# Output projection by Strassen's scheme, token-major, with its sum transposed and x added by VectorE; all 22 inner blocks of down in the scheme

## The chip, the cores and the metric

One core of one Trainium2 chip. Five engines matter: TensorE (PE; PEld is its weight load), VectorE (DVE), ScalarE (ACT), GpSimd (POOL) and SyncE (SP), whose queue issues most DMAs. The metric is device microseconds of one launch.

## What is computed

One decoder layer for 512 tokens, model width 1024, FFN width 2816. The reference, cut to what matters here (the head splits and the two attentions are left out):

```python
h = rms_norm(x, g_mix[layer])
proj = h @ w_in[layer]
...
g = jax.nn.sigmoid(gates + b_gate[layer]).reshape(b, s, N_BRANCHES, D_MODEL)
merged = g[:, :, 0] * (ya @ w_branch_a[layer]) + g[:, :, 1] * (yb @ w_branch_b[layer])
x = x + merged @ w_out[layer]
h = rms_norm(x, g_ffn[layer])
u = causal_depthwise_conv(h @ w_up[layer], conv_w[layer], conv_b[layer])
u_gate, u_val = jnp.split(u, 2, axis=-1)
x = x + (jax.nn.silu(u_gate) * u_val) @ w_down[layer]
return rms_norm(x, g_final)
```

## The kernel before

Every large product is made of three fp32r matmuls, hi by hi, hi by lo, lo by hi (`mm3`, L71 to L74). Weights come as tiles of 128 x 1024 fp32 (`raw`, five buffers, on SP's queue); ScalarE copies the high half (`whi`), VectorE subtracts the low half (`wlo`): `wload` L55 to L69, `split_w` L602 to L609, `split_out` (L262, L263) for activations.

Stages: input projection, the two attentions, then per output block of 128 features the gate projections (16 blocks, held back as fillers for TensorE, L452) and the two gated products `ab` (`mm<-ya`, `mm<-yb`, L496 to L504). Their sum is split into `m`.

**Output projection** (L512 to L527): feature-major, for each of 8 output blocks 8 inner blocks x 3 matmuls of 512 columns into one PSUM bank. VectorE adds the bank to x (`x1T`, L516); ScalarE and VectorE make the halves of `h2` (L517, L518); ScalarE stores x1 to DRAM (L520) and squares it (L522), VectorE adds the squares up (L526). Behind the first up block eight passes against a vector of ones sum the squares over the features (L117).

**Up** (L532 to L590): 44 blocks of 24 matmuls, two to each of the 22 inner blocks (FT). Per block: VectorE's product with the norm's factor (`u`, L559), ScalarE's first tap (L561), VectorE's two other taps (L562, L564). Of a pair of inner blocks (j) the first 9 (NP) go to `tm` and `xb`, four sums and a split into `xa`, the left operands of a Strassen scheme (L576 to L582); the last four inner blocks (18 to 21) go to `gT` unchanged (L569).

**Down**, token-major, eight PSUM banks of 128 tokens x 512 features (c11 to c22, each two blocks of 128 tokens). First pass, per j of 9: two weight loads, two subtractions (L620, L621), a copy (L622), two splits, and the four products c22, c21, c11, c12 of 6 matmuls each. Then the sums u2, u3 (L650 to L661). Second pass, per j: a subtraction (L642), a weight split, the splits of `xs` and `w4` (L263), prepared two steps ahead, and three products of 6. At j = 6 the residual x1, read back from DRAM feature-major (`x1R`), is added by 32 transposes on TensorE (L684). Then 96 plain matmuls for `gT`, 128 tokens after 128 tokens, each half followed by its ending: Square with row sum (L699), product with the gain (L701), square root (L704), reciprocal and corrections, scaling (L712, L714), store (L715).

TensorE's order is that of the code (`manual_schedule`); a scheduler orders the instructions of the other engines. A buffer's next writer waits for its last reader.

Of the kernel before, what the change touches and what calls it, by code (L numbers as in the profile page):

```python
# [10 lines left out]
F32 = mybir.dt.float32  # L11
# [16 lines left out]
NP = 9  # L28
# [3 lines left out]
          + [("out", i) for i in range(KT)] + [("up", i, b) for i in range(FT) for b in range(2)]  # L32
# [6 lines left out]
def trunk_layer(ctx: ExitStack, tc: tile.TileContext, xT: bass.AP, w: bass.AP, vec: bass.AP,  # L39
# [46 lines left out]
    warmb = consts.tile([128, 448], BF, name="warmb")  # L86
    nc.vector.memset(warmb, 0.0)
# [55 lines left out]
    xp = pool(st1, "xp", 6)  # L143
    p1 = pool(st1, "p1", 1, PSUM)
# [471 lines left out]
    for j in range(NP):  # L616
# [9 lines left out]
        if j == NP - 1:  # L626
            steps = steps[2:] + steps[1::-1]
# [155 lines left out]
```

## Time and profile before

| | |
|---|---|
| median of 3 runs | 731.37 us (731.29 to 731.92) |
| the profiled execution | 731.76 us, span 730.0 us |
| granted TensorE clock, mean | 0.997 |
| PE / PEld / DVE / ACT / POOL busy | 722.6 / 601.0 / 511.1 / 326.7 / 22.9 us |
| chain that ended last | PE 99% |
| DMA | 80.95 MB, mean 111 GB/s |

Busy time is read as a share of the span; the chain of waits is followed back from the last instruction, at each step to what released it. A matmul of 512 columns lasts 0.39 us in the trace and overlaps the next; what counts is the distance between starts. Durations below are of the profiled execution.

### The profile page before, as it was taken

What the parts mean: (1) busy time and instruction counts of PE and PEld (TensorE: products, weight loads), DVE (VectorE), ACT (ScalarE), POOL (GpSimd) and SP (SyncE); (2) the same over time, 40 slices, a digit from 0 to 9 for tenths busy, and PEclk for the clock granted to TensorE, in tenths of its full rate; (3) what the DMA queues carried; (4) which work ended last, traced back from release to release, by engine and by line L of the source; (5) the groups of instructions that cost most, each with busy time, mean ns of one, the idle gap of its engine ahead of it and who ended that gap; (6) DMA issues with size and microseconds to landing.
All of it is one profiled execution on the core that took longest, in us unless ns stands there. A gap on an engine that the chain in (4) does not pass through costs nothing.

```text
span 730.0 us, 9687 instructions
## 1 busy us (share of the span) xinstructions
PE 722.6 (99%) x3836; PEld 601.0 (82%) x3836; DVE 511.1 (70%) x724; ACT 326.7 (45%) x468; POOL 22.9 (3%) x40
## 2 busy tenths in 40 slices
PE   9999999999999999999999999999999999999996
PEld 6887889889888888888888888888888888888885
DVE  7778866693963644446548788877778888889913
ACT  6335544563663323224335444434444445466623
POOL 0000000320410000000000000000000000000000
PEclk9999999999999999999999999999999999999998
DMA  8422111021225232233432232232232223568303
GB/s 310 186 87 87 58 59 59 30 88 58 85 91 173 89 113 87 92 110 125 147 132 87 86 115 88 87 116 87 91 112 87 95 79 115 193 216 294 105 1 115
DMA packets 25389, 80.95 MB, mean 111 GB/s; under 512 B 2816, under 2 KB 3456, under 8 KB 25344
## 3 DMA queue, kind: packets, MB, share of 16 engines
q1 hardware_dynamic: 23472, 77.06, 31.3%
q10 hardware_dynamic: 1872, 3.28, 1.2%
q8 instruction: 30, 0.49, 0.3%
q14 instruction: 15, 0.12, 0.0%
HBM read 76.13 MB, written 4.19 MB: 110 GB/s over the span
## 4 chain that ended last, share of the span: by engine, by line
PE 99%; DVE 0%; issue 0%; ACT 0%; DVEq 0%; ACTq 0%
PE mm L72 24%; PE mm L74 23%; PE mm L73 23%; PE c L72 5%; PE c L74 5%; PE c L73 5%; PE q L187 3%; PE tp L428 2%; PE tp L406 2%; PE sc L329 1%; PE sc L339 1%; PE mm L149 0%; PE v L74 0%; PE v L72 0%; PE v L73 0%; PE c L684 0%
## 5 line engine op out<-in xcount | busy, mean ns | idle before, releaser
L67 ACT ACTIVATE whi<-raw 128x1024 fp32r<-128x1024 f32 (+2 forms) x106 | 106.9, 1012 | 212.3 <-PE mm L73 130.9
L72 PE MATMUL mm<-h,whi 128*128 128x512 f32 x352 | 137.1, 390 | 0.0
L74 PE MATMUL mm<-h,wlo 128*128 128x512 f32 x352 | 137.0, 389 | 0.0
L73 PE MATMUL mm<-h,whi 128*128 128x512 f32 x352 | 136.9, 389 | 0.0
L68 DVE TENSOR_TENSOR wlo<-raw,whi 128x1024 fp32r<-128x1024 f32 (+2 forms) x106 | 122.8, 1163 | 15.8 <-ACT whi L67 15.5
L72 PE MATMUL mm<-xg,whi 128*128 128x512 f32 x224 | 90.0, 402 | 0.0
L74 PE MATMUL mm<-xg,wlo 128*128 128x512 f32 x224 | 87.5, 390 | 0.0
L73 PE MATMUL mm<-xg,whi 128*128 128x512 f32 x224 | 87.3, 390 | 0.0
L73 PEld LDWEIGHTS mm<-h,whi 128*128 128x128 f32 x352 | 66.1, 188 | 13.8
L74 PEld LDWEIGHTS mm<-h,wlo 128*128 128x128 f32 x352 | 66.1, 188 | 13.7
L72 PEld LDWEIGHTS mm<-h,whi 128*128 128x128 f32 x352 | 66.1, 188 | 13.6
L559 DVE TENSOR_TENSOR u<-mm,rb 128x512 f32<-128x512 f32 x44 | 30.3, 691 | 30.5 <-PE mm L74 30.4
L72 PEld LDWEIGHTS mm<-xg,whi 128*128 128x128 f32 x224 | 42.1, 188 | 10.2 <-issue 1.8
L74 PEld LDWEIGHTS mm<-xg,wlo 128*128 128x128 f32 x224 | 42.0, 188 | 9.1
L73 PEld LDWEIGHTS mm<-xg,whi 128*128 128x128 f32 x224 | 42.2, 188 | 7.8
L607 ACT ACTIVATE whi<-raw 128x1024 fp32r<-128x1024 f32 x31 | 31.9, 1050 | 23.5 <-DVE raw L620 14.3
L608 DVE TENSOR_TENSOR wlo<-raw,whi 128x1024 fp32r<-128x1024 f32 x31 | 37.3, 1220 | 3.6 <-ACT whi L607 3.6
L561 ACT ACTIVATE t<-u,vecs 128x512 f32<-128x512 f32 x44 | 35.2, 803 | 2.0 <-DVE u L559 2.0
L452 DVE TENSOR_TENSOR g<-mm,rb 128x512 f32<-128x512 f32 x16 | 11.0, 688 | 34.4 <-PE mm L74 34.4
L564 DVE SCALAR_TENSOR_TENSOR t<-u,vecs,t 128x510 f32<-128x510 f32 x44 | 32.9, 749 | 1.3
L562 DVE SCALAR_TENSOR_TENSOR t<-u,vecs,t 128x511 f32<-128x511 f32 x44 | 32.8, 747 | 1.4 <-ACT t L561 1.3
L567 ACT ACTIVATE t<-t 128x512 f32<-128x512 f32 x22 | 13.8, 628 | 35.5 <-DVE t L564 35.5
(202 smaller groups left out, 1271.9 us busy)
## 6 DMA issues: line engine op xcount, KB each, us to landing
raw<-w SPq DMA_DIRECT2D x127, 512.0 KB, 3.3
xk<-xT SPq DMA_DIRECT2D x8, 256.5 KB, 5.3
x1T<-xT SPq DMA_DIRECT2D x8, 256.0 KB, 5.0
x1D<-x1T ACTq DMA_DIRECT2D x8, 256.0 KB, 2.0
x1R<-x1D SPq DMA_DIRECT2D x4, 512.0 KB, 7.5
raw<-w SPq DMA_DIRECT2D x6, 256.0 KB, 5.5
out<-on ACTq DMA_DIRECT2D x4, 256.0 KB, 2.5
out<-on SPq DMA_DIRECT2D x4, 256.0 KB, 2.7
```

Of the source, the lines that this page charges most:

```text
L67: nc.scalar.activation(hi[:, sl], raw[:, sl], AF.Copy)
L68: nc.vector.tensor_sub(lo[:, sl], raw[:, sl], hi[:, sl].bitcast(F32))
L72: nc.tensor.matmul(ps, a[0], b[0], start=start, stop=False, **kw)
L73: nc.tensor.matmul(ps, a[0], b[1], start=False, stop=False, **kw)
L74: nc.tensor.matmul(ps, a[1], b[0], start=False, stop=stop, **kw)
L187: nc.tensor.matmul(qk0[c], w0[i][:, (k % 2) * 512 + c * 128:(k % 2) * 512 + (c + 1) * 128], xg[k][:, j], start=(k == 0 and n == 0), stop=( ...
L559: nc.vector.tensor_mul(u, ps, rb2)
L561: nc.scalar.activation(t, u, AF.Identity, bias=cb[:, c:c + 1], scale=cw[:, 2, c:c + 1])
L562: nc.vector.scalar_tensor_tensor(t[:, 1:], u[:, :S - 1], cw[:, 1, c:c + 1], t[:, 1:], op0=OP.mult, op1=OP.add)
L564: nc.vector.scalar_tensor_tensor(t[:, 2:], u[:, :S - 2], cw[:, 0, c:c + 1], t[:, 2:], op0=OP.mult, op1=OP.add)
L607: nc.scalar.activation(hi, raw, AF.Copy)
L608: nc.vector.tensor_sub(lo, raw, hi.bitcast(F32))
```

## The change

The output projection takes the scheme that down has, in pairs of inner blocks (HP = 4): `a_side` makes `oa` and `ob` from the gated sums, `first_pass` and `sums` are shared with down, the second pass is written out, c12's products last. The result is token-major in eight banks (`po`). x comes in token-major (a new input) and VectorE adds it (`x1_add`); `x1_turn` transposes 256 tokens x 512 features back (8 transposes a time) and ScalarE and VectorE make `h2` from PSUM. The squares are summed by ScalarE token by token (`x1_sq`). x1 is stored by SP's queue. In down all 11 pairs are in the scheme, `gT` and the plain matmuls are gone, VectorE adds the residual (`residual`), and the last three steps (NL) of the second pass are held: c21's 18 matmuls, the endings of tokens 256 to 511, then the four other banks, 9 matmuls each, with their endings. `u` has one buffer instead of two, small constants move to other pools, and `spare` takes the place of the pool `ptr2`, with no tile taken from it.

```diff
-NP = 9
+NP = FT // 2
+NL = 3
...
+    warmb = xp.tile([128, 448], BF, name="warmb", bufs=1)
+    nc.vector.memset(warmb, 0.0)
...
-    ptr = pool(psB, "ptr2", 2, PSUM)
+    spare = pool(psB, "spare", 2, PSUM)
     pmm = pool(psB, "pmm2", 6, PSUM)
...
+    def a_side(odd, put, tm, xa, xb):
+        if not odd:
+            put(tm[:, 0::4])
+            return
+        put(xb[:, 0::2])
+        nc.vector.tensor_add(tm[:, 1], tm[:, 4], xb[:, 2])
+        nc.vector.tensor_sub(tm[:, 3], tm[:, 0], tm[:, 4])
+        nc.vector.tensor_sub(tm[:, 2], tm[:, 1], tm[:, 0])
+        nc.vector.tensor_sub(xb[:, 1], xb[:, 0], tm[:, 2])
+        split_out(xa.rearrange("p a b c -> p a (b c)"), tm[:, :4].rearrange("p b c -> p (b c)"))
...
-        nc.vector.tensor_add(g[0], g[0], g[1])
-        split_out(mhl[i], g[0])
+        if i % 2 == 0:
+            tm = mtp.tile([128, 5, 256], F32, name="tm")
+        g0, g1 = (u.rearrange("p (t c) -> p t c", t=2) for u in g)
+        a_side(i % 2, lambda dst: nc.vector.tensor_add(dst, g0, g1), tm, oxa[i // 2], oxb[i // 2])
...
-    for i in range(KT):
-        wo = wload(("out", i))
-        ps = pmm.tile([128, S], F32, name="mm")
-        for k in range(KT):
-            mm3(ps, blk(wo, k), (mhl[k][:, 0], mhl[k][:, 1]), k == 0, k == KT - 1)
-        nc.vector.tensor_add(x1T[i], x1T[i], ps)
-        nc.scalar.activation(h2[i][:, 0], x1T[i], AF.Copy, scale=gffn[:, i:i + 1])
...
+    for t in range(QT):
+        nc.sync.dma_start(x1[:, t], x[t * 128:(t + 1) * 128])
...
+    for j in range(HP):
+        first_pass(oq, j, HP, oxa[j], (("ox", j), ("out", 2 * j)), t2[j], slots[j], True)
...
+    second = [oprep(j, (wsp, osp, osp)[j]) for j in range(3)]
+    w4s = [oprep4(j) for j in range(2)]
+    last, lact = sums(oq, ocb)
...
+    def x1_add(t, h):
+        sl = slice(h * 512, (h + 1) * 512)
+        ins = nc.vector.tensor_add(x1[:, t, sl], x1[:, t, sl], oq[f"c{t // 2 + 1}{h + 1}"][t % 2])
+        nc.sync.dma_start(x1D[t][:, sl], x1[:, t, sl])
+        return ins
+
+    def x1_turn(T, h):
+        q = oq[f"c{T + 1}{h + 1}"]
+        for i in range(4):
+            for t in range(2):
+                o = (i % 2) * 256 + t * 128
+                nc.tensor.transpose(q[i // 2][:, o:o + 128],
+                                    x1[:, 2 * T + t, h * 512 + i * 128:h * 512 + (i + 1) * 128], ident)
+        for i in range(4):
+            k = 4 * h + i
+            src = q[i // 2][:, (i % 2) * 256:(i % 2 + 1) * 256]
+            hl = h2[k][:, :, T * 256:(T + 1) * 256]
+            act = nc.scalar.activation(hl[:, 0], src, AF.Copy, scale=gffn[:, k:k + 1])
+            dve = nc.vector.scalar_tensor_tensor(hl[:, 1], src, gffn[:, k:k + 1], hl[:, 0].bitcast(F32),
+                                                 op0=OP.mult, op1=OP.subtract)
+        return dve, act
+
+    def x1_sq(t, h):
+        nc.scalar.activation(sqj, x1[:, t, h * 512:(h + 1) * 512], AF.Square, accum_out=sums2[:, h, t:t + 1])
+
+    for j in range(HP):
...
+        if j == 1:
+            for t in range(2):
+                with tc.issue_after(last.ins):
+                    last = nc.vector.tensor_add(oq["c22"][t], oq["c22"][t], oq["u3", t])
+            for t in (2, 3):
+                with tc.issue_after(last.ins):
+                    last = x1_add(t, 1)
+        prod(oq["c11"], xs, 0, wa, 0, False, j == HP - 1, skip_group_check=True)
+        prod(oq["c21"], xs, 2, w4, 0, False, j == HP - 1, skip_group_check=True)
+        if j == 2:
+            x1_turn(1, 1)
+    for T in range(2):
+        for t in range(2):
+            x1_add(2 * T + t, 0)
+    for t in range(2):
+        for j, (xs, wa) in enumerate(second):
+            mm3(oq["c12"][t], tuple(xs[:, c, 1, t * 128:(t + 1) * 128] for c in range(2)), blk(wa, 1, 512),
+                False, j == HP - 1, skip_group_check=True)
+        if t == 0:
+            for T in range(2):
+                x1_turn(T, 0)
+        x1_add(t, 1)
...
-    ups = [up_mm()]
-    r2 = rstd_cols(ssq2, ptr, "tp", "n2")
-    ups.append(up_mm())
+        u0, u1 = (up_mm(wload(("up",) + upq.pop(0))) for _ in range(2))
+    for k in range(4):
+        ups = [next(u0)]
+    last, lact = x1_turn(0, 1)
+    for k in range(4):
+        ups.append(next(u1))
+    ups = [ups[0], ups[1]]
+    for u in (u0, u1):
+        for _ in u:
+            pass
+    for t in range(QT):
+        for h in range(2):
+            x1_sq(t, h)
...
-        if i >= NX:
-            nc.vector.tensor_mul(uc[0], uc[0], uc[1])
-            split_out(gT[i], uc[0])
-            continue
...
+    def residual(t, h):
+        return nc.vector.tensor_add(acc[t, h], acc[t, h], x1R[:, t, h * 512:(h + 1) * 512])
...
+        if j < NP - NL:
+            prod(cq["c11"], xs, 0, wa, 0, False, False, skip_group_check=True)
+            prod(cq["c21"], xs, 2, w4, 0, False, False, skip_group_check=True)
+            prod(cq["c12"], xs, 1, wa, 1, False, False, skip_group_check=True)
+        else:
+            held.append((xs, wa, w4))
...
-        if j == NP - 3:
-            for t in range(QT):
...
-                        nc.tensor.matmul(acc[t, h][:, i * 128:(i + 1) * 128],
-                                         x1R[2 * h + i // 2][:, i % 2, t * 128:(t + 1) * 128], ident,
-                                         is_transpose=True, start=False, stop=False, skip_group_check=True)
...
+    for n, (xs, wa, w4) in enumerate(held):
+        prod(cq["c21"], xs, 2, w4, 0, False, n == NL - 1, skip_group_check=True)
+    for t in (2, 3):
+        residual(t, 0)
+        for n, h in enumerate((1, 0)):
+            ending(t, n, h, fss[t])
+    for t in (0, 1):
         for h in range(2):
...
+            for n, (xs, wa, w4) in enumerate(held):
+                mm3(acc[t, h], tuple(xs[:, c, h, t * 128:(t + 1) * 128] for c in range(2)), blk(wa, h, 512),
+                    False, n == NL - 1, skip_group_check=True)
+            ending(t, h, h, fss[t])
```

Three places show how the order moves. First TensorE, at the first gated product (`mm<-ya`), behind the last gate projection (`mm<-xg`); a row in brackets names the engine whose semaphore it waits for. Before:

```order
L73 MATMUL mm<-xg_107,whi 128x512
L74 MATMUL mm<-xg_107,wlo 128x512
L72 MATMUL mm<-ya_93,whi 128x512
L73 MATMUL mm<-ya_93,whi 128x512
L74 MATMUL mm<-ya_93,wlo 128x512 [waits DVE_49]
```

And now:

```order
L74 MATMUL mm<-xg_99,whi 128x512
L75 MATMUL mm<-xg_99,wlo 128x512
L73 MATMUL mm<-ya_85,whi 128x512 [waits DVE_49]
L74 MATMUL mm<-ya_85,whi 128x512
L75 MATMUL mm<-ya_85,wlo 128x512
```

The wait on VectorE moved from the product's third matmul to its first.

Second VectorE between the sums of the output projection and the first turn (L587 is the last of the sums, L264 a lower half, L596 the subtraction in `oprep`, L552 a weight's lower half, L647 c22 plus u3, L613 the addition of x); b0 and b1 are c22's banks:

```order
L587 TENSOR_TENSOR b2_3172<-b0_3170,u20_3409 128x512
L587 TENSOR_TENSOR b3_3173<-b1_3171,u21_3413 128x512
L264 TENSOR_TENSOR w4_3425<-ot2_3198,w4_3425 128x512
L596 TENSOR_TENSOR ot3_3199<-raw_3440,ot3_3199 128x512
L264 TENSOR_TENSOR xs_3443<-ob3_2500,xs_3443 128x768
L552 TENSOR_TENSOR wlo_3447<-raw_3440,whi_3446 128x1024
L264 TENSOR_TENSOR w4_3450<-ot3_3199,w4_3450 128x512
L647 TENSOR_TENSOR b0_3170<-b0_3170,p1s0_3416 128x512
L647 TENSOR_TENSOR b1_3171<-b1_3171,p1s1_3419 128x512
L613 TENSOR_TENSOR x1_3203<-x1_3203,b0_3170 128x512
L613 TENSOR_TENSOR x1_3203<-x1_3203,b1_3171 128x512
```

Before, VectorE's work for a block of the output projection was this, with nothing behind it that TensorE waited for until up:

```order
L516 TENSOR_TENSOR x1T_2512<-x1T_2512,mm 128x512
L68 TENSOR_TENSOR wlo<-raw,whi 128x1024
L518 SCALAR_TENSOR_TENSOR h_3180<-x1T_2512,vecs,h_3180 128x512
L526 TENSOR_TENSOR ssq_3182<-ssq_3182,sq_3446 128x512
L516 TENSOR_TENSOR x1T_2513<-x1T_2513,mm 128x512
```

The addition of x, once the first thing done with a bank, now stands behind nine other instructions, and the transposes behind it.

Third VectorE where up ends and down's first pass begins (the last up block's `u`, its taps, and the weight splits of down's first two steps). Before:

```order
L621 TENSOR_TENSOR raw<-raw 128x512
L559 TENSOR_TENSOR u_5278<-mm,rb_3487 128x512
L608 TENSOR_TENSOR wlo<-raw,whi 128x1024
L562 SCALAR_TENSOR_TENSOR t_5280<-u_5278,vecs,t_5280 128x511
L564 SCALAR_TENSOR_TENSOR t_5280<-u_5278,vecs,t_5280 128x510
L569 TENSOR_TENSOR t_5243<-t_5243,t_5280 128x512
L263 TENSOR_TENSOR gT_3580<-t_5243,gT_3580 128x512
L608 TENSOR_TENSOR wlo<-raw,whi 128x1024 x2
```

And now:

```order
L565 TENSOR_TENSOR raw<-raw 128x512
L717 TENSOR_TENSOR u_5393<-b_5368,rb_3189 128x512
L552 TENSOR_TENSOR wlo<-raw,whi 128x1024
L720 SCALAR_TENSOR_TENSOR t_5395<-u_5393,vecs,t_5395 128x511
L722 SCALAR_TENSOR_TENSOR t_5395<-u_5393,vecs,t_5395 128x510
L729 TENSOR_TENSOR xb_3731<-t_5358,t_5395 128x2x256
L489 TENSOR_TENSOR tm<-tm,xb_3731 128x256
L491 TENSOR_TENSOR tm<-tm 128x256
L492 TENSOR_TENSOR xb_3731<-xb_3731,tm 128x256
L264 TENSOR_TENSOR xa_3747<-tm,xa_3747 128x1024
L552 TENSOR_TENSOR wlo<-raw,whi 128x1024 x2
```

The sums and the wider split of a Strassen pair stand where the plain split of `gT` stood, ahead of the same two weight splits.

## Rows read from the trace of the kernel before

**Rows 1.** The page: the span, and each engine's busy time (share of the span) and instructions.
```profile
span 730.0 us, 9687 instructions
PE 722.6 (99%) x3836; PEld 601.0 (82%) x3836; DVE 511.1 (70%) x724; ACT 326.7 (45%) x468; POOL 22.9 (3%) x40
```
**Rows 2.** The page: the chain that ended last, by engine.
```profile
PE 99%; DVE 0%; issue 0%; ACT 0%; DVEq 0%; ACTq 0%
```
**Rows 3.** Windows of the output projection, of down's first pass and of its second: length, busy time (instructions) of PE, PEld, DVE, ACT, POOL, granted clock, DMA share, GB/s.
```profile
328.00:371.80 43.80, 43.80 (x195) 36.26 (x194) 25.09 (x32) 17.12 (x24) 0.00 (x0) 1.00 0.40 139
...
612.60:661.50 48.90, 48.90 (x217) 40.50 (x216) 41.75 (x45) 27.35 (x34) 0.00 (x0) 1.00 0.62 203
661.50:702.00 40.50, 40.50 (x196) 33.79 (x195) 30.93 (x39) 21.32 (x27) 0.00 (x0) 1.00 0.40 145
```
**Rows 4.** Instructions by tile, the output projection's first kind of matmul: duration in ns (least, median, most), first and last start in us.
```profile
L72 PE MATMUL mm<-m,whi x64: 389/389/389, 328.3 to 371.1; 128*128 128x512 f32 x64
```
**Rows 5.** The same view of down's banks: the transposes of x1, and the first kind of the plain matmuls.
```profile
L684 PE MATMUL c<-ident,x1R x32: 272/273/273, 690.3 to 693.7; 128*128 128x128 f32 x32
...
L72 PE MATMUL c<-whi,gT x32: 389/389/389, 702.0 to 723.1; 128*128 128x512 f32 x32
```
**Rows 6.** Timeline behind the first up block: start, duration, engine, line. The ones passes' weight loads, and the next matmul.
```profile
376.99 1.08 PEld L117 LDWEIGHTS tp<-ones,ssq 128*128 128x128 f32 x8
...
378.02 0.49 PE L72 MATMUL mm<-h,whi 128*128 128x512 f32 x1
```
**Rows 7.** Timeline at the first gated product.
```profile
230.34 0.39 PE L72 MATMUL mm<-ya,whi 128*128 128x512 f32 x1
...
230.53 0.69 DVE L452 TENSOR_TENSOR g<-mm,rb 128x512 f32<-128x512 f32 x1 [1.61 <-PE mm L74]
```
**Rows 8.** VectorE's groups by line and shape: count, busy us, mean ns of one, idle us before them and its releasers.
```profile
L608 DVE TENSOR_TENSOR wlo<-raw,whi 128x1024 fp32r<-128x1024 f32 x31 | 37.3, 1220 | 3.6 <-ACT whi L607 3.6
...
L562 DVE SCALAR_TENSOR_TENSOR t<-u,vecs,t 128x511 f32<-128x511 f32 x44 | 32.8, 747 | 1.4 <-ACT t L561 1.3
...
L263 DVE TENSOR_TENSOR xs<-xb,xs 128x768 fp32r<-128x768 f32 x9 | 8.5, 950 | 0.0
...
L642 DVE TENSOR_TENSOR t<-raw,t 128x512 f32<-128x512 f32 x9 | 6.2, 683 | 0.7 <-DMA raw<-w 0.7
...
L516 DVE TENSOR_TENSOR x1T<-x1T,mm 128x512 f32<-128x512 f32 x8 | 5.5, 688 | 16.9 <-PE mm L74 16.9
...
L580 DVE TENSOR_TENSOR tm<-tm 128x256 f32<-128x256 f32 x9 | 3.8, 425 | 0.3
```
**Rows 9.** VectorE's timeline in down's first pass (the first two) and its second: start, duration, and in brackets the idle time before it and its releaser.
```profile
632.16 1.23 DVE L620 TENSOR_TENSOR raw<-raw 128x1024 f32<-128x1024 f32 x1 [1.72 <-DMA raw<-w]
...
642.65 1.23 DVE L620 TENSOR_TENSOR raw<-raw 128x1024 f32<-128x1024 f32 x1 [0.82 <-DMA raw<-w]
...
678.00 0.68 DVE L642 TENSOR_TENSOR t<-raw,t 128x512 f32<-128x512 f32 x1
...
681.21 0.68 DVE L642 TENSOR_TENSOR t<-raw,t 128x512 f32<-128x512 f32 x1
```
**Rows 10.** ScalarE's groups by line and shape, columns as in rows 8.
```profile
L607 ACT ACTIVATE whi<-raw 128x1024 fp32r<-128x1024 f32 x31 | 31.9, 1050 | 23.5 <-DVE raw L620 14.3 <-PE mm L73 8.9 <-DMA raw<-w 0.3
...
L262 ACT ACTIVATE w<-t 128x512 fp32r<-128x512 f32 x9 | 5.6, 621 | 2.3 <-DVE t L642 2.3
...
L699 ACT ACTIVATE junk<-c 128x512 f32<-128x512 f32 x8 | 4.8, 599 | 23.5 <-PE c L74 23.0 <-ACT on L712 0.5
...
L699 ACT ACTIVATION_READ_ACCUMULATOR junk<-c 128x1 f32 x8 | 1.6, 194 | 0.0
...
L704 ACT ACT_TABLE_LOAD x1 | 1.3, 1283 | 0.0
...
L704 ACT ACTIVATE fs<-fs 128x1 f32<-128x1 f32 x4 | 1.2, 294 | 0.1
```
**Rows 11.** Timeline of TensorE and VectorE where down begins.
```profile
612.55 0.39 PE L72 MATMUL c<-whi,xa 128*128 128x512 f32 x1
...
612.98 0.68 DVE L559 TENSOR_TENSOR u<-mm,rb 128x512 f32<-128x512 f32 x1
...
618.76 2.36 DVE L608 TENSOR_TENSOR wlo<-raw,whi 128x1024 fp32r<-128x1024 f32 x2 [0.26 <-ACT whi L607]
```
**Rows 12.** Timeline of TensorE and ScalarE at the end.
```profile
723.52 0.39 PE L74 MATMUL c<-whi,gT 128*128 128x512 f32 x1
...
724.01 0.60 ACT L699 ACTIVATE junk<-c 128x512 f32<-128x512 f32 x1 [1.88 <-PE c L74]
...
725.70 0.72 ACT L712 ACTIVATE on<-on,fs 128x512 f32<-128x512 f32 x1 [0.68 <-DVE fs L708]
```
**Rows 13.** DMA issues from 600 to 665 us: count, KB each, median us to landing.
```profile
raw<-w SPq DMA_DIRECT2D x21, 512.0 KB, 4.3
x1R<-x1D SPq DMA_DIRECT2D x4, 512.0 KB, 7.5
```
**Rows 14.** Windows around down's transposes, columns as in rows 3.
```profile
690.00:694.00 4.00, 4.00 (x36) 3.86 (x35) 2.85 (x4) 0.00 (x0) 0.00 (x0) 1.00 0.00 0
694.00:698.00 4.00, 4.00 (x19) 3.28 (x18) 0.00 (x0) 0.00 (x0) 0.00 (x0) 1.00 0.00 0
```
**Rows 15.** TensorE's timeline at the start of the span: the warm-up, nine matmuls of 448 columns and one of 128.
```profile
1.22 3.65 PE L149 MATMUL mm<-warmb 128*128 128x448 bf16 x10 [1.22 <-DVE warmb L87]
```

More of the change, by code (lines that the diff above doesn't have):

```diff
@@ L502, in trunk_layer, with bank @@
             nc.vector.tensor_mul(g[b], g[b], ps)
-        nc.vector.tensor_add(g[0], g[0], g[1])
-        split_out(mhl[i], g[0])
-    ysta.close()
+        if i % 2 == 0:
+            tm = mtp.tile([128, 5, 256], F32, name="tm")
+        g0, g1 = (u.rearrange("p (t c) -> p t c", t=2) for u in g)
+        a_side(i % 2, lambda dst: nc.vector.tensor_add(dst, g0, g1), tm, oxa[i // 2], oxb[i // 2])
+    tst.close()
+    ysta.close()
+    psB.close()
+    psB = ExitStack()
+    po = pool(psB, "po", 1, PSUM)
+    def bank(n):
+        return po.tile([128, 512], F32, name=f"b{n}")
+    oq = {n: [bank(2 * i + t) for t in range(2)] for i, n in enumerate(("c22", "c12", "c21", "c11"))}
     hst = ExitStack()
@@ new lines, in prod, with first_pass @@
+    def prod(bank, a, b, wt, h, start, stop, **kw):
+        for t in range(2):
+            sl = slice(t * 128, (t + 1) * 128)
+            mm3(bank[t], (a[:, 0, b, sl], a[:, 1, b, sl]), blk(wt, h, 512), start, stop, **kw)
+    def first_pass(cq, j, n, xa, keys, t2, pools, last):
+        r0 = rload(keys[0])
+        r1 = rload(keys[1])
+        r2 = wraw.tile([128, 1024], F32, name="raw")
+        nc.vector.tensor_sub(r2, r0, r1)
+        nc.vector.tensor_sub(r1[:, 512:], r0[:, 512:], r2[:, :512])
+        nc.scalar.activation(t2, r1[:, 512:], AF.Copy)
+        w2 = split_in(pools[0], r2)
+        w1 = split_in(pools[1], r1)
+        steps = [("c22", 1, w2, 0), ("c21", 3, w2, 1), ("c11", 0, w1, 0), ("c12", 2, w1, 1)]
+        if j == n - 1 and last:
+            steps = steps[2:] + steps[1::-1]
+        for m, b, wt, h in steps:
+            prod(cq[m], xa, b, wt, h, j == 0, j == n - 1)
@@ L542, in trunk_layer @@
+    with tc.issue_after(last.ins), tc.issue_after(lact.ins):
+        u2 = up_mm(wload(("up",) + upq.pop(0)))
+    bcast_rows(r2, po, "b6", rb2)
+    ups.append([*u2][-1])
+    ost.close()
     mst.close()
-    NX = 2 * NP
     gp = pool(ctx, "gp", 1)
-    gT = {k: gp.tile([128, 2, S], F32R, name=f"gT{k}") for k in range(NX, FT)}
     xb = [gp.tile([128, 3, 256], F32, name=f"xb{j}") for j in range(NP)]
@@ L634, in trunk_layer @@
     x1q = pool(ctx, "x1q", 1)
-    x1R = [x1q.tile([128, 2, S], F32, name=f"x1R{k}") for k in range(KT // 2)]
+    x1R = x1q.tile([128, QT, D], F32, name="x1R")
     fin = pool(ctx, "fin", 1)
@@ L687, in trunk_layer @@
+        if j < QT:
+            nc.sync.dma_start(x1R[:, j], x1D[j])
+        if j == QT:
+            nc.sync.dma_start(gb, gfin[None, :].to_broadcast([128, D]))
+            for t in (2, 3):
+                with tc.issue_after(last.ins):
+                    last = residual(t, 1)
+    for t in range(2):
+        for h in range(2):
+            with tc.issue_after(last.ins), tc.issue_after(filled[-1].ins):
+                last = residual(t, h)
     with tc.issue_after(last.ins):
         nc.vector.tensor_scalar(gb, gb, -0.5, None, op0=OP.mult)
-    wl = [split_w(rload(("down", k))) for k in range(NX, FT)]
```

228 lines of the change are left out of this document (111 added, 117 removed).

## The prediction

> **What bounds the kernel now.** The page comes first. TensorE is busy for 722.6 of 730.0 us [rows 1], and the chain of waits gives it 99% of the span [rows 2]; VectorE (511.1) and ScalarE (326.7) have time over. So the time is the number of TensorE's instructions by their pitch, plus the few places where it waits. The windows by stage say where another engine comes close [rows 3]: in the output projection VectorE works 25.09 of 43.80 us, in down's first pass 41.75 of 48.90, in its second 30.93 of 40.50. The change hands VectorE more work in all three, so each place where its result is waited for is gone through below.
>
> An execution takes more than its span: the profiled one took 731.76 us for a span of 730.0. The sum is made against 731.76, which is 0.39 above the median of 731.37.
>
> **TensorE's gain.** The old output projection issues a matmul of one kind, every third, from 328.3 to 371.1 [rows 4]: 42.8 over 63 x 3 = 189 steps is 0.2265 us each. Down's plain matmuls give 0.2269 (702.0 to 723.1 over 93 steps, [rows 5]); 0.2266 is taken.
> - Output projection: 8 x 8 x 3 = 192 become 4 x 24 + 4 x 18 = 168. 24 x 0.2266 = **-5.4**.
> - Down: 9 x 42 + 96 = 474 become 11 x 42 = 462. 12 x 0.2266 = **-2.7**.
> - The 32 transposes go from down (690.3 to 693.7, [rows 5]), and 32 of the same shape come in before up: 0.
> - The sum of squares no longer goes through TensorE. The eight ones passes start with a weight load at 376.99, and the next matmul at 378.02 [rows 6], where its place was one pitch on, at 377.22, with some 0.1 of a slow restart: **-0.9**. ScalarE's eight Squares replace them, during the first up blocks, in ScalarE's idle time.
>
> Together -9.0.
>
> **What is newly waited for.**
>
> (a) *Head of the gated products.* PSUM banks are renumbered, since no tile is taken from the spare pool. The first product now goes into the bank of the last gate, so its first matmul carries the wait (first order fence). Before, that matmul ran at 230.34, while VectorE read the gate from 230.53 for 0.69 [rows 7]. It must now run after 231.22 plus a handover of some 0.1: **+1.0** (0.9 to 1.1). Nothing hides it, since TensorE's order is fixed.
>
> (b) *First turn.* The transposes of token blocks 2 and 3 stand behind j = 2 of the second pass. They need x added to c22, and VectorE gets there only through a chain (second order fence): w4's lower half 0.68, a subtraction 0.68, that of xs 0.95, that of a weight 1.22, w4's again 0.68, two sums and two additions of x at 0.69, together 6.97 [rows 8], less eight overlaps of 0.08 (678.00 to 681.21 is 3.21 a step, where the four durations add to 3.54, [rows 9]): 6.3. ScalarE's half of the w4 split (0.62, [rows 10]) and three handovers of 0.1 lie on it too: 7.2. TensorE has 24 matmuls to cover it, 5.4: **+1.8**. If VectorE starts the chain an operation early, 0.5; if two ScalarE copies of 1.05 stand ahead of w4's, 4.
>
> (c) *First up block* waits for the lower halves of h2, written by eight VectorE pieces of 256 at 0.42 [rows 8], 3.4 us, against 12 matmuls (2.7) and the first up matmuls: **+0.4** (0, if they keep up, to 1.3, if the two additions of x stand in between).
>
> (d) *Start of down.* Up's last pair is now a Strassen pair too, so VectorE puts seven more operations ahead of down's second weights (third fence). Before, TensorE began down at 612.55, and the split that begins at 618.76 ended its first half at 619.98, 7.4 later [rows 11]. Now the row is u 0.69, a split 1.22, two of 0.75, a product 0.69, four of 0.42, and two splits of 1.22 [rows 8]: 8.2, begun 0.43 after TensorE's start as before (612.98), so done at 8.7. TensorE wants these weights for j = 1's third product, after 36 matmuls, 8.2; with a handover of 0.1: **+0.6** (0, if overlaps of 0.08 between nine operations hold, to 1.9, one more split).
>
> (e) *Late weights* at the end of first and second pass, where two more steps run than before. A first-pass step costs VectorE 3 x 1.22 + 0.69 = 4.35, against 24 matmuls, 5.44; a second-pass step 3.21 against 18, 4.08. About 1 us is in hand each: **+0.2** (0, to 2.5 if the idle 1.72 and 0.82 of [rows 9] fall on the last steps).
>
> (f) *Tail.* Before, the last matmul ends at 723.91, the Square follows at 724.01, the last scaling ends at 726.42, and a store ends the span at 730.0, 6.1 behind the last matmul [rows 12]. Now the endings of four blocks of 128 tokens stand beside the last 36 matmuls, 8.2 us: on ScalarE seven Squares with their read-out (0.60 + 0.19), a table load of 1.28, four square roots of 0.29 [rows 10] and two scalings of 0.72 are 9.4 ahead of the last Square. With four handovers of 0.1 it comes late by **+1.6** (0.5, if the roots and scalings fall behind it, to 4, if VectorE's parts of the endings, 0.69 and 0.75 each, hold ScalarE up five times); the old tail's own length stays.
>
> (g) *Head.* The warm-up's memset now stands third on VectorE: **+0.1**.
>
> The eight residual additions that replace down's transposes (8 x 0.69 = 5.5) lie on VectorE in the second pass, which has 9.6 to spare [rows 3], and six run before the held products: 0 on TensorE; if that cover were gone, (f) holds their price.
>
> Sum of waits: 1.0 + 1.8 + 0.4 + 0.6 + 0.2 + 1.6 + 0.1 = +5.7. Net 5.7 - 9.0 = -3.3 against 731.76, 728.5 for an execution like the profiled one, and with 0.39 off **728.1** as the median.
>
> **Rivals.**
>
> *A. Loads pace down's first pass.* In the trace VectorE's first operation of a step waits for a weight from DMA: 1.72 at 632.16, 0.82 at 642.65, in every second step [rows 9]. 512 KB loads take 4.3 us at that time [rows 13]. Were it 1.72 in each of 11 steps: 4.35 + 1.72 less four overlaps of 0.08 is 5.75, above 5.44; 0.31 x 11 = +3.4, **731.5**, no difference. Against it: TensorE did not wait in these steps before. 15%.
>
> *B. Waits mostly hidden.* If VectorE runs ahead of the order's worst case, (b) and (f) fall to 0.5 each, (c) to (e) to 0.2 together: +2.3, **724.7**. For it: in 700 us the old kernel shows almost no such wait. Against: (a) is certain, and the tail's ScalarE work is in the rows. 10%.
>
> *C. x arrives late: slower.* The four loads of x stand on SP behind the second up weight, which needs the raw buffer of the ninth of the twelve output weights (five buffers), which comes free after some three of the four first-pass steps, 3 x 5.44, say 17 us into the stage. The same 4 x 512 KB as x1R take 7.5 [rows 13], so they land at about 25. VectorE adds token blocks 2 and 3 at about 30 (96 + 36 matmuls), so some 4 us are in hand. Past that each us is a us of TensorE at the first turn. From 5 us past, at 35, it is slower than before: **733.1**. Against it: that wants loads of over 17 us. 7%.
>
> *D. The clock falls behind transposes.* In this trace the stretch with 32 transposes shows granted clock 1.00, and the stretch behind it too [rows 14]; that is the 2.4 GHz level. By this row, 0. Half pace is seen once, in the warm-up: 3.65 us for 9 x 448 + 128 = 4160 columns, 0.88 ns each [rows 15], against 0.2266 / 512 = 0.44; so a matmul of 512 at the lower pace costs 0.22 more, and 24 of them behind a turn and its wait +5.3: **733.4**. The Trainium skill, "TensorE: Matmul & The Clock Gate", Part 4, says of transposes by TensorE that they do not count as busy for the clock in the way matmuls do; by it the turns, three of which stand next to a wait, would bring this on. The trace speaks against it, though there no wait stood beside the transposes. 4%.
>
> That the scheme does not remove what it says is excluded: the order has the 24 and 12 fewer.
>
> **How the numbers follow.** The forecast, 728.1 with 726 to 730 as its own range, has 60%. A reaches to 731.5, and (b) or (f) at its upper end to 731; so the range is 725 to 732. It leaves out half of B, and C, D and the upper ends together (4%). What a measurement of this kernel can tell from no change is 0.2%, 1.5 us: faster is below 729.9, slower above 732.8. Faster: 60 + 10 = 70%. Same: A and part of the upper ends, 15 + 3 = 18%. Slower: C, D and the rest, 12%.
>
> **What would show it.** Right: 168 matmuls of the output projection and 462 of down at 0.2266; no ones passes after the first up block; TensorE idle for 1.0 before the first gated product, about 1.8 before the first turn, about 0.6 in down's second step; some 7.7 us from the last matmul's end to the span's, where it was 6.1; granted clock 1.00 throughout. Wrong: idle time of TensorE in every first-pass step of down (A), VectorE's first addition of x waiting for DMA (C), pitches near 0.44 behind a turn (D), or a sum of TensorE's waits far from 5.7, above all at the first turn and in the tail, the two terms with the widest bounds.

## The result and the profile after

The changed kernel takes 728.05 us (median of 4 runs, 727.26 to 728.54), the kernel before 731.33 on the same chip: ratio 0.9948, 95% interval 0.9935 to 0.996. 728.1 was forecast, with 725 to 732 as the range and 70% on faster, which the prediction sets below 729.9. The profiled execution took 728.18, against 731.76 of the one before: 3.58 less, where the sum of the prediction says 3.3.

The page after: span, busy times, and the chain by engine, which answer to [rows 1] and [rows 2].

```profile
span 726.4 us, 9745 instructions
PE 715.2 (98%) x3792; PEld 593.4 (82%) x3792; DVE 554.3 (76%) x795; ACT 346.9 (48%) x506; POOL 22.7 (3%) x40
PE 93%; DVE 4%; ACT 2%; issue 1%; DMA 1%; ACTq 0%; DVEq 0%
```

TensorE still bounds it, with 7.4 us less work, but the chain now leaves it for VectorE and ScalarE in places; VectorE does 43 us more. What TensorE waited for, in the changed kernel: line and releaser, sum, times, longest.

```profile
PE mm L145 <- DVE R L375: 1.3, 1, 1.3
PE b L622 <- DVE x L613: 1.3, 2, 1.0
PE mm L73 <- DVE g L453: 0.8, 1, 0.8
PE c L74 <- DVE wlo L552: 0.4, 1, 0.4
PE b L74 <- DVE h L629: 0.3, 1, 0.3
```

Apart from the first row (the warm-up's memset, 1.22 before), these are the terms (b), (a), (d) and (c) in the order of their size, each at the place named. TensorE's timeline at three of them: start, duration, and in brackets the idle time and its releaser.

```profile
230.82 0.39 PE L75 MATMUL mm<-xg,wlo 128*128 128x512 f32 x1
231.99 0.50 PE L73 MATMUL mm<-ya,whi 128*128 128x512 f32 x1 [0.78 <-DVE g L453]
...
359.78 0.39 PE L75 MATMUL b<-w,xs 128*128 128x512 f32 x1
361.18 0.33 PE L622 MATMUL b<-ident,x 128*128 128x128 f32 x1 [1.01 <-DVE x L613]
361.77 0.98 PE L622 MATMUL b<-ident,x 128*128 128x128 f32 x7 [0.27 <-DVE x L613]
362.51 0.48 PE L73 MATMUL b<-whi,xs 128*128 128x512 f32 x1
...
622.00 0.39 PE L73 MATMUL c<-whi,xa 128*128 128x512 f32 x1
622.78 0.50 PE L74 MATMUL c<-wlo,xa 128*128 128x512 f32 x1 [0.40 <-DVE wlo L552]
```

A wait costs more than the idle time in brackets, since starts count: from 230.82 to 231.99 is 1.17 where a pitch is 0.23, and the next start came 0.34 later, not 0.23. So (a) cost 1.05, (b) 1.65 (2.73 from 359.78 to 362.51, where a matmul and eight transposes take 1.08), (d) 0.66.

By stage, from starts in the two profiles: the new output projection lasts 42.47 us (330.08 to 372.55) where the old one lasted 43.52; down, from its first matmul to the end of its last, 105.57 (613.84 to 719.41) where it was 111.36; the tail behind that 7.0 where it was 6.1.

### The profile page after: what moved, and what is told of

Same layout as the page of the kernel before. It is cut to its first block, busy times and chain, and to the rows that moved or that the text cites. A ratio compares the mean times of both kernels' runs of the same rounds, so it can differ in the third digit from the quotient of the medians.

```text
span 726.4 us, 9745 instructions
## 1 busy us (share of the span) xinstructions
PE 715.2 (98%) x3792; PEld 593.4 (82%) x3792; DVE 554.3 (76%) x795; ACT 346.9 (48%) x506; POOL 22.7 (3%) x40
## 4 chain that ended last, share of the span: by engine, by line
PE 93%; DVE 4%; ACT 2%; issue 1%; DMA 1%; ACTq 0%; DVEq 0%
PE b L74 12%; PE b L75 12%; PE b L73 12%; PE mm L73 11%; PE mm L75 11%; PE mm L74 11%; PE c L74 4%; PE c L75 4%; PE c L73 4%; PE q L188 3%; PE tp L429 2%; PE tp L407 2%; PE sc L330 1%; PE sc L340 1%; DVE wlo L552 1%
## 5 line engine op out<-in xcount | busy, mean ns | idle before, releaser
L74 PE MATMUL b<-h,whi 128*128 128x512 f32 x352 | 137.1, 389 | 0.3 <-DVE h L629 0.3
L73 PE MATMUL b<-h,whi 128*128 128x512 f32 x352 | 137.1, 390 | 0.0
L75 PE MATMUL b<-h,wlo 128*128 128x512 f32 x352 | 136.9, 389 | 0.0
L69 DVE TENSOR_TENSOR wlo<-raw,whi 128x1024 fp32r<-128x1024 f32 (+2 forms) x98 | 112.8, 1157 | 14.1 <-ACT whi L68 13.8
L74 PEld LDWEIGHTS b<-h,whi 128*128 128x128 f32 x352 | 66.1, 188 | 14.4 <-DVE h L629 0.7
L75 PEld LDWEIGHTS b<-h,wlo 128*128 128x128 f32 x352 | 66.1, 188 | 13.7
L73 PEld LDWEIGHTS b<-h,whi 128*128 128x128 f32 x352 | 66.1, 188 | 13.6
L551 ACT ACTIVATE whi<-raw 128x1024 fp32r<-128x1024 f32 x45 | 46.7, 1052 | 32.7 <-DVE raw L564 19.6
L552 DVE TENSOR_TENSOR wlo<-raw,whi 128x1024 fp32r<-128x1024 f32 x45 | 54.4, 1219 | 4.4 <-ACT whi L551 4.4
L717 DVE TENSOR_TENSOR u<-b,rb 128x512 f32<-128x512 f32 x44 | 30.3, 691 | 30.4 <-PE b L75 30.3
L74 PE MATMUL c<-wlo,xa 128*128 128x512 f32 x88 | 34.3, 390 | 0.4 <-DVE wlo L552 0.4
L73 PE MATMUL c<-whi,xa 128*128 128x512 f32 x88 | 34.2, 389 | 0.0
L75 PE MATMUL c<-whi,xa 128*128 128x512 f32 x88 | 34.2, 389 | 0.0
```

The lines of the kernel that those rows point to most:

```text
L69: nc.vector.tensor_sub(lo[:, sl], raw[:, sl], hi[:, sl].bitcast(F32))
L73: nc.tensor.matmul(ps, a[0], b[0], start=start, stop=False, **kw)
L74: nc.tensor.matmul(ps, a[0], b[1], start=False, stop=False, **kw)
L75: nc.tensor.matmul(ps, a[1], b[0], start=False, stop=stop, **kw)
L551: nc.scalar.activation(hi, raw, AF.Copy)
L552: nc.vector.tensor_sub(lo, raw, hi.bitcast(F32))
```

## The experiments

All times are medians of 5 runs (experiment 4: 11, the two combinations: 4, the kernel before in 9: one run). Beside the first eight the kernel before took 731.52 us, beside the last two (7 and the second combination) 731.46. A stage's length is taken from starts in the profiles, which agree to 0.1 us where nothing was changed, so the trace settles what the medians alone could not.

**1. The banks as before.**

```diff
     spare = pool(psB, "spare", 2, PSUM)
+    for _ in range(2):
+        spare.tile([128, 512], F32, name="tp")
```

> Two tiles are taken from the spare pool, so the gated products get the banks that they had in the kernel before. Theory: TensorE's wait at the first gated product (start 1.17 behind the last gate's where a pitch is 0.23, and a slow restart of 0.11: 1.05 us in all) goes and nothing takes its place, so 728.05 - 1.05 = 727.0 us. Rival: the gated products or the first pass of the output projection wait for VectorE somewhat later instead, since its work there is unchanged: TensorE's idle time moves behind 232 us and the time stays at 728.0.

726.55 us, ratio 0.9934 (0.9921 to 0.9947). From the first value projection to the first gated product 202.32 us passed, with the change 203.21, before 202.33; from there to the output projection 97.92, with the change 98.09, before 97.92. Together 1.06 less, and no wait has come up behind it: the theory holds, and what the medians differ by beyond that (1.5 in all) lies within the scatter of the start, in 9.

**2. The first turn behind the fourth step.**

```diff
-        if j == 2:
+        if j == 3:
             x1_turn(1, 1)
```

> The first turn (token blocks 2 and 3, features 512 to 1023) is put behind the last of the four second-pass steps, not the third, so 12 more matmuls (2.7 us) stand ahead of it. Theory: its wait for VectorE's addition of x, 1.65 us with restarts, lies under them and nothing else changes: 728.05 - 1.65 = 726.4 us. Rival: the wait moves. The halves of h2 that this turn feeds, 8 pieces on ScalarE and 8 on VectorE at 0.42, now fall together with those of the next two turns; TensorE then waits for h2 at the first up blocks, where it waited 0.5 us, for 1 to 1.5 us more: 727.5 to 728.0 us.

726.62 us, ratio 0.9935 (0.9921 to 0.9949). The output projection lasts 40.75 us instead of 42.47: 1.72 less. The rival has a small part: at the first up block TensorE's delay for h2 is 0.64, where it was 0.53. The theory holds for the wait; but the tail is 7.7 us here (716.94 to 724.6), 0.7 longer, with another order of ScalarE's endings, as in 7 below. So from the first value projection to the end it is 0.8 us shorter, where the medians differ by 1.4; the rest is of the size of the scatter of the start (27.80 us here, 28.78 in the changed kernel).

**3. The table loaded early.**

```diff
         if n == 0:
+            if t == 2:
+                nc.scalar.activation(fs[:, 4:5], fs[:, 0:1], AF.Sqrt)
```

> One more square root of a single column, its result unused, is put behind the first Square of the endings (695.8 us), so that the table of 1.28 us is loaded there and not among the endings of the last 8 us. Theory: ScalarE's queue sets the tail (last Square 0.37 behind the last matmul, last scaling behind another one); with 1.28 us taken from its row the tail goes from 7.0 to between 6.4 and 6.7 us: 727.4 to 727.7 us. Rival: VectorE's small operations and the stores set the tail, and it stays at 7.0: 728.05 us.

727.75 us, ratio 0.9946 (0.9933 to 0.9959): by the medians no difference. The tail is 6.7 us (719.50 to 726.2) where it was 7.0: at the edge of the theory where it gains least. The last Square:

```profile
719.60 0.60 ACT L810 ACTIVATE junk<-c 128x512 f32<-128x512 f32 x1 [0.80 <-PE c L75]
```

It now waits for TensorE alone, 0.10 behind the last matmul's end where it was 0.37: that is the 0.3. So ScalarE's row is what made the last Square late; it is not the other 0.6 of the longer tail, since the last scaling follows the Square by 2.09, as in the changed kernel (2.08).

**4. The old output projection under the new down.** The sections of before for the projection, the sum of squares and the banks, and the transposes in down:

```diff
+        wo = wload(("out", i))
...
+            mm3(ps, blk(wo, k), (mhl[k][:, 0], mhl[k][:, 1]), k == 0, k == KT - 1)
...
+        if j == NP - NL - 1:
...
+                        nc.tensor.matmul(acc[t, h][:, i * 128:(i + 1) * 128],
+                                         x1R[2 * h + i // 2][:, i % 2, t * 128:(t + 1) * 128], ident,
...
-        residual(t, 0)
```

> The output projection, the sum of squares, the banks and the 32 transposes in down as before; all 11 pairs of down in the scheme and its last three steps held, as after. Theory (the sum of the trace): against the changed kernel it has 24 matmuls (5.44) and the ones passes (0.9) more, and the waits at the gated products (1.05), the first turn (1.65) and the first up block (0.53) less; the 32 transposes stand in another place at the same price: 728.05 + 6.34 - 3.23 = 731.2 us, so down's part alone gives back nearly all of its 2.7. Rival: the longer tail comes from VectorE's eight additions of the residual, which are gone here; then the tail is 6.1, not 7.0 us, and the time 730.3.

730.05 us, ratio 0.9978 (0.9969 to 0.9987): the theory's 731.2 fails, the rival's 730.3 is near. The tail is 6.4 us, neither the theory's 7.0 nor the rival's 6.1. Its last matmul ends at 721.73; ScalarE's endings behind it:

```profile
721.88 0.60 ACT L706 ACTIVATE junk<-c 128x512 f32<-128x512 f32 x1 [0.42 <-PE c L75]
...
723.57 0.72 ACT L722 ACTIVATE on<-on,fs 128x512 f32<-128x512 f32 x1 [0.68 <-DVE fs L716]
```

The last Square now waits for TensorE alone, and the last scaling follows it by 1.69, as in [rows 12] (724.01 to 725.70); in the changed kernel it is 2.08 (719.78 to 721.86). So two thirds of the longer tail are gone with VectorE's additions; experiment 5 moves only two of them. Down alone is worth 1.5 us by the medians (731.52 to 730.05) and the rest of the change about 2 (ratios 0.9978 and 0.9948): of 6.3 us of matmuls and ones passes in the output projection, 3.2 went to waits and 0.6 to the tail, which leaves 2.5, as from the first value projection to the end (697.6 us in the changed kernel, 700.1 here).

**5. The residual of c21 early.**

```diff
-            for t in (2, 3):
-                with tc.issue_after(last.ins):
-                    last = residual(t, 1)
+        if j in (QT, QT + 1):
+            for t in (2, 3):
+                with tc.issue_after(last.ins):
+                    last = residual(t, QT + 1 - j)
...
-        residual(t, 0)
```

> VectorE adds the residual to c21's two banks after the sixth second-pass step, not behind the held products, so c21's endings can start when its last matmul ends (711.1 us in the trace of the changed kernel, where the first of its Squares ran at 712.68). Theory: the 1.3 us of additions ahead of c21's endings are what piles ScalarE's and VectorE's endings up; the tail goes from 7.0 to the 6.4 us that it has with the old output projection, and the time to 727.4 us. Rival: TensorE waits for the two additions in the middle of the second pass (1.4 us between c21's products of two steps, 2.7 us apart, on a VectorE that is 98% busy there), the gain in the tail is lost there, and the time is 728.0 or up to 728.8 us.

727.14 us, ratio 0.9938 (0.9924 to 0.9951). Tail 6.3 us (719.43 to 725.7), second pass 0.2 longer (45.23, not 45.04): 0.5 in all. The theory holds, with a little of the rival. The last Square there, 0.03 behind the last matmul's end, with the last scaling 1.69 behind it:

```profile
719.46 0.60 ACT L811 ACTIVATE junk<-c 128x512 f32<-128x512 f32 x1 [0.57 <-PE c L75]
```

**6. A subtraction of the last pair on GpSimd.**

```diff
-        nc.vector.tensor_sub(xb[:, 1], xb[:, 0], tm[:, 2])
+        eng.tensor_sub(xb[:, 1], xb[:, 0], tm[:, 2])
...
+               nc.gpsimd if i == FT - 1 else nc.vector)
```

> Of the last Strassen pair of up, the one subtraction that only the second pass needs (0.42 us) runs on GpSimd, not on VectorE. Theory: TensorE's wait for the low half of the weights of down's second step (0.40 us idle, 0.66 with the slow restart) is VectorE's row of operations there, so it shrinks by 0.4 of row time: 727.4 to 727.6 us. Rival: the row is held up by something ahead of it (the weight's load, or ScalarE's half of the split), and TensorE waits as long as before: 728.05 us.

728.0 us, ratio 0.9949 (0.9937 to 0.9962), and TensorE's wait is 0.40 us as before: the rival. VectorE's low half of the last pair's split, in the changed kernel and then here:

```profile
620.37 1.23 DVE L264 TENSOR_TENSOR xa<-tm,xa 128x1024 fp32r<-128x1024 f32 x1 [0.67 <-ACT xa L263]
```
```profile
619.30 1.23 DVE L264 TENSOR_TENSOR xa<-tm,xa 128x1024 fp32r<-128x1024 f32 x1 [1.13 <-ACT xa L263]
```

The 0.42 taken out only became idle time (0.67 to 1.13): VectorE waits there for ScalarE's high half.

**7. That split in two halves.** So the copy of 1.06 us on ScalarE was cut:

```diff
-        split_out(xa.rearrange("p a b c -> p a (b c)"), tm[:, :4].rearrange("p b c -> p (b c)"))
+        n = 4 // parts
+        for i in range(parts):
+            sl = slice(i * n, (i + 1) * n)
+            split_out(xa[:, :, sl].rearrange("p a b c -> p a (b c)"), tm[:, sl].rearrange("p b c -> p (b c)"))
```

> The left operand of up's last Strassen pair is split in two halves of 512 columns, on ScalarE and VectorE, not in one piece of 1024; nothing else. In the trace of the changed kernel VectorE stands idle for 0.67 us there until ScalarE's copy of 1.06 us is done, behind which the weights of down's second step come, 0.40 us late. Theory: this handover, not the sum of VectorE's operations, sets the wait; with halves ScalarE starts some 0.5 us earlier and VectorE's idle time falls to 0.2 or less, so TensorE's wait (0.40, 0.66 with restart) goes: 727.4 us. Rival: ScalarE's copy of the weight, which stands behind, sets it (1.05 us, ended at 621.29): then the two halves, a fixed cost of 0.2 longer on ScalarE, leave the wait at 0.4 or more: 728.05 us or a little above.

```profile
619.59 1.29 DVE L264 TENSOR_TENSOR xa<-tm,xa 128x512 fp32r<-128x512 f32 x2
```

No idle time ahead of it, none of TensorE either; down's first pass lasts 59.99 us instead of 60.53. The theory holds for the wait. But the time does not move (727.6 us, ratio 0.9948, 0.9936 to 0.9961): the tail is 7.6 us where it was 7.0. Its last matmul ends at 718.84; ScalarE behind it:

```profile
718.59 0.71 ACT L830 ACTIVATE on<-on,fs 128x512 f32<-128x512 f32 x1
719.33 0.34 ACTq L831 DMA_DIRECT2D out<-on  x1
719.72 0.60 ACT L814 ACTIVATE junk<-c 128x512 f32<-128x512 f32 x1 [0.42 <-ACT on L830]
...
720.30 0.71 ACT L830 ACTIVATE on<-on,fs 128x512 f32<-128x512 f32 x1
720.92 0.28 ACT L820 ACTIVATE fs<-fs 128x1 f32<-128x1 f32 x1
```

A scaling and its store stand ahead of the last Square, which comes 0.88 behind the last matmul, and another scaling ahead of the last square root: the scheduler has put the endings in another order. What was won ahead of the crowded tail was lost in it here, and in part in 2, where the order changed too; not in 1, where the tail stayed at 7.0.

**8. All places in one kernel**, first with the subtraction on GpSimd for (d):

> The banks as before, the first turn behind the fourth step, the table loaded early, the residual of c21 early, and the subtraction on GpSimd, all in one kernel. Theory (the places are independent, each is idle time of TensorE or of the tail): 728.05 - 1.05 - 1.65 - 0.6 - 0.5 = 724.2 us, which is 9.0 less than before but for what is left of the waits, some 2 us. Rival: they are not independent, since VectorE, once TensorE runs 2.7 us earlier in the output projection, comes late at the next place instead (first up block, down's first pass): 725.5 us or more.

723.94 us, ratio 0.9897 (0.9883 to 0.991): the rival's 725.5 fails. That the theory's 724.2 is met so closely is in part luck: from the first value projection to the end the kernel is 3.2 us shorter than the changed one, not 3.8, since TensorE still waits 0.40 for (d), as in 6; the profiled run's start was 0.9 earlier (27.91). Then with the halves in its place:

> The banks as before, the first turn behind the fourth step, the table loaded early, the residual of c21 early (these four without the subtraction on GpSimd), and the split of the last pair in halves. Theory: to the 723.9 us measured for the kernel with all places but this one the halves add their 0.6: 723.3 us. Rival: the halves do nothing here (the wait is set by the weight), and it stays at 723.9.

723.58 us (723.37 to 723.90, where the other had 723.75 to 724.10), ratio 0.9891 (0.9876 to 0.9907): from the first value projection to the end, 693.98 us against 694.39, the halves bring 0.4 of the 0.6, and the tail stays at 6.3 us. By the times alone the two kernels, run on two chips, are hardly told apart. It is the fastest kernel run, and beats the kernel before by 7.9 us, of 9.0 that the matmuls give. The view of TensorE's waits names only the warm-up's memset:

```profile
PE mm L145 <- DVE R L375: 1.3, 1, 1.3
```

What is too short for that view is still there: at the first up block two starts come 0.44 and 0.56 behind the one ahead, so (c) costs 0.65 here.

```profile
369.35 0.39 PE L75 MATMUL b<-h,wlo 128*128 128x512 f32 x1
369.79 0.49 PE L73 MATMUL b<-h,whi 128*128 128x512 f32 x1
370.35 0.50 PE L74 MATMUL b<-h,whi 128*128 128x512 f32 x1
370.69 0.39 PE L75 MATMUL b<-h,wlo 128*128 128x512 f32 x1
```

**9. The kernel before once more.**

> The kernel before once more, for its first 28 us. In the profiles up to now the first value projection begins at 28.01 us (before), 28.04, 28.51, 27.80, 28.79 (kernels with the changed start) and 28.78 (the changed kernel). Theory: this is the landing of the first loads, which varies from execution to execution, so the old kernel scatters by several tenths too. Rival: the memset that now stands third costs it, and the old kernel is at 28.0 again.

Its first value projection starts at 28.31 us, 0.3 behind the same kernel's first profile:

```profile
28.31 0.39 PE L72 MATMUL v<-whi,xg 128*128 128x512 f32 x1
```

The ten profiles with the changed start are at 27.68 to 28.79 (mean 28.3), the two of before at 28.01 and 28.31. The changed kernel's 28.78 is at the late end of this scatter. In it the first loads were issued at the same time as before (0.80), and ScalarE's first copy of a weight began at 4.61 where it was 4.33. With two profiles of the old start, a difference of a few tenths stays open; one of 0.8 is not shown.

But the theory's cause, the landing of the loads, covers only a part of it. TensorE's first matmuls behind the warm-up, in the first profile of the kernel before and then in the changed kernel:

```profile
4.80 2.50 PE L187 MATMUL q<-xg,whi 128*128 128x512 f32 x8
7.13 1.07 PE L187 MATMUL q<-xg,wlo 128*128 128x512 f32 x4
8.04 1.52 PE L187 MATMUL q<-xg,whi 128*128 128x512 f32 x6
```
```profile
5.08 2.98 PE L188 MATMUL q<-xg,whi 128*128 128x512 f32 x8
7.89 1.09 PE L188 MATMUL q<-xg,wlo 128*128 128x512 f32 x4
8.82 0.62 PE L188 MATMUL q<-xg,whi 128*128 128x512 f32 x2
```

The first starts 0.28 later, as the copy does. Then the same 12 matmuls, with no wait among them, take 3.74 us and not 3.24 (2.72 by the pitch): the first of them still run at about the warm-up's half pace (starts at 5.67, 6.10 and 6.53 in the changed kernel, 0.43 apart). They are 0.23 apart from 6.44 in the kernel before and from 7.43 in the changed one; from 8.04 and 8.82 on the two run alike. In the ten profiles with the changed start, whose warm-up begins at 1.30 in each, the first of these matmuls stands at 4.83 to 5.08, and from there to the first value projection 22.81 to 23.95 us pass. So most of the scatter lies behind the first loads; what sets the end of the half pace stays open.

## Why the prediction was right

Each term, as forecast and as the profile has it:

| | forecast | measured | shown by |
|---|---|---|---|
| matmuls, ones passes, transposes | -9.0 | -9.2 | stages, as the rest |
| (a) bank of the last gate | +1.0 | +1.05 | experiment 1 |
| (b) first turn | +1.8 | +1.65 | experiment 2 |
| (c) first up block | +0.4 | +0.5 | trace only |
| (d) start of down | +0.6 | +0.66 | experiment 7 |
| (e) late weights | +0.2 | 0 | trace only |
| (f) tail | +1.6 | +0.9 | experiments 3, 4, 5 |
| (g) start of the span | +0.1 | +0.8 | experiment 9: scatter |

The first row is no measurement of its own: from the first value projection to the end of the last matmul the changed kernel takes 690.63 us, the kernel before 695.90, and the 5.27 between them and the 3.9 of (a) to (d) make 9.2. With it the terms sum to -3.6, by which the spans differ. In the last row only 0.08 is the memset's (the warm-up begins at 1.30, before at 1.22); the rest is the start's scatter.

(b) was right in its mechanism and its parts. VectorE's chain and ScalarE's half ahead of it, in the changed kernel:

```profile
354.76 0.63 ACT L263 ACTIVATE w<-ot 128x512 fp32r<-128x512 f32 x1 [2.37 <-PE b L75]
```
```profile
355.43 0.69 DVE L264 TENSOR_TENSOR w<-ot,w 128x512 fp32r<-128x512 f32 x1 [2.53 <-ACT w L263]
...
359.25 1.29 DVE L647 TENSOR_TENSOR b<-b,p1s 128x512 f32<-128x512 f32 x2
360.44 1.27 DVE L613 TENSOR_TENSOR x<-x,b 128x512 f32<-128x512 f32 x2
```

From 355.43 to 361.71 are 6.28 us, where 6.3 was worked out. The chain starts where it does because ScalarE's copy waits for TensorE to release one of the two w4 buffers (2.37 idle): that makes VectorE's 6.3 against TensorE's 5.4 a wait and not a lead.

**(d)** came out near for the wrong reason. The sum of VectorE's durations (8.2, done 8.7 after TensorE's start) met the measured 8.89 (613.84 to 622.73), but it held no wait for ScalarE: begun 0.20 after TensorE, not 0.43, VectorE stood idle for 0.20 and 0.67 for ScalarE's halves, and taking 0.42 of its own work away gained nothing.

In **(f)**, too large by 0.7, the step "on ScalarE seven Squares ... are 9.4 ahead of the last Square" failed. With four handovers that made 9.8 us, in the 8.2 of the last 36 matmuls. The changed kernel's tail, TensorE's first of these matmuls, ScalarE and then VectorE:

```profile
711.09 0.39 PE L73 MATMUL c<-whi,xs 128*128 128x512 f32 x1
```
```profile
695.78 0.58 ACT L810 ACTIVATE junk<-c 128x512 f32<-128x512 f32 x1
...
712.68 0.60 ACT L810 ACTIVATE junk<-c 128x512 f32<-128x512 f32 x1 [4.63 <-DVE c L775]
713.18 0.19 ACT L810 ACTIVATION_READ_ACCUMULATOR junk<-c 128x1 f32 x1
...
719.78 0.58 ACT L810 ACTIVATE junk<-c 128x512 f32<-128x512 f32 x1
...
720.49 0.30 ACT L816 ACTIVATE fs<-fs 128x1 f32<-128x1 f32 x1
...
721.86 0.72 ACT L826 ACTIVATE on<-on,fs 128x512 f32<-128x512 f32 x1 [0.47 <-DVE fs L820]
```
```profile
711.96 1.29 DVE L775 TENSOR_TENSOR c<-c,x1R 128x512 f32<-128x512 f32 x2
...
720.56 0.74 DVE L824 SCALAR_TENSOR_TENSOR on<-c,fs,gb 128x512 f32<-128x512 f32 x1
721.22 0.15 DVE L818 RECIPROCAL fs<-fs 128x1 f32<-128x1 f32 x1
```

ScalarE's row there is only 7.10 us long (712.68 to 719.78): one of the seven Squares ran long before, at 695.78, the last of the four roots comes behind the last Square, and ScalarE's operations overlap as VectorE's do (the read-out at 713.18 starts 0.10 before the Square's end), which the sum took off in (b) but not here. On the other side the row starts 1.6 into the stretch, since its first Square waits for VectorE's last two additions of the residual. So the last Square comes 0.37 behind the last matmul's end (719.41), not 0.1.

The tail's 0.9 has three parts. The late Square is 0.27. The last scaling follows it by 2.08 and not 1.69, 0.39 more: the last reciprocal starts 0.43 behind the root's end, behind VectorE's scaling of the block before, where it was 0.03. And from the last scaling's end to the span's end 3.82 us pass, before 3.58; it is 3.79 to 3.85 in all ten kernels with the new down, and no run here shows why. The prediction put the residual additions at 0, with "if that cover were gone, (f) holds their price"; experiment 5 moved the two of them that stood behind c21's held products, and 0.7 of the 0.9 went with them.

(f) was too large by 0.7 and (g) too small by as much, and (g) is mostly scatter: that the total came out nearer than its parts is luck.

The rivals. **A**: TensorE waits in down's first pass for nothing but (d): its 264 matmuls take 60.53 us, less 0.66 a pitch of 0.2268. **B**: (b) and (d) were there in full. **C**: the four loads of x were issued at 346.51, 16.4 us into the stage (17 were worked out), over 2.05 us, and took 7.3 us each, so they were there 24 to 26 us into it (25); VectorE added x at 360.44, at 30.4 (30), straight behind its sums and with no idle time ahead.

```profile
346.51 2.05 SPq L540 DMA_DIRECT2D x<-x  x4
```

**D**: the granted clock is 1.00, the 2.4 GHz level, in the windows with the first turn and behind it. Their columns are those of [rows 3]; the first row is the window of the warm-up.

```profile
1.00:5.00 4.00, 3.65 (x10) 1.34 (x10) 1.29 (x10) 1.67 (x3) 0.68 (x4) 1.00 0.69 217
361.00:364.00 3.00, 2.56 (x15) 2.11 (x16) 3.00 (x5) 0.91 (x2) 0.00 (x0) 1.00 0.71 247
364.00:368.00 4.00, 4.00 (x19) 3.32 (x18) 3.95 (x8) 1.59 (x4) 0.00 (x0) 1.00 0.91 280
368.00:370.00 2.00, 2.00 (x18) 1.93 (x17) 1.17 (x2) 1.30 (x4) 0.00 (x0) 1.00 1.03 383
```

That column alone would not settle it, since it reads 1.00 for the warm-up at half pace too. The pitch does: behind the first turn matmuls start at 362.82, 363.06 and 363.29, behind the next two at 370.05, 370.28 and 370.51, 0.23 apart. (Half pace was not seen in the warm-up alone, as D says, but in the first matmuls behind it as well, in 9.)

The rule of the Trainium skill ("TensorE: Matmul & The Clock Gate", Part 4), that transposes do not count as busy for the clock as matmuls do, changed nothing here: behind 8 transposes next to 1.65 us of waits, and behind 16 more some 6 us later, the granted clock is 1.00 and the pitch 0.23.

## What to carry to other kernels

Where one engine has 99% of the chain, count its instructions by their pitch and then go along its new order and ask at every producer that moved: how long is that engine's queue from the last release to this result, and what covers it. Each delay but (c) has its own cheap edit (a bank, a step later, an addition earlier, a split in halves), which won back 3.6 us together by the stages, of the 4.8 that the change gave away behind the start; but look for the producer's own idle time before taking work off it, since a handover between two engines is not in the sum of either one's durations. Open the tail first: in two of the edits a crowded one took part or all of what was won ahead of it.

## What the runs showed of the hardware that was not expected

- The instruction behind a wait is slow as well: after the waits (a), (c) and (d) the second start comes 0.33 to 0.34 us later instead of 0.23 (231.99 to 232.33, 373.89 to 374.22, 622.78 to 623.12), so such a wait costs 0.1 us beyond its idle time. Behind a row of transposes with no wait it is much the same (0.32, from 369.73 to 370.05).
- The start scatters by 1.1 us from execution to execution (27.68 to 28.79 at the first value projection), as much as some of the edits here; only 0.3 of it shows in the start of the first matmul behind the warm-up (4.80 to 5.08), and in the two profiles compared in 9 the rest is a slower pace of the next matmuls, without a wait. Stages compared by starts within a profile were good to 0.1 us.
- Transposes of 128 x 128 fp32 follow each other at 0.10 us (16 from 368.07 to 369.73), while one lasts 0.27 in the trace, at the full granted clock.
